# A hybrid S5 and mLSTM decoder block: rotation tables of the state space built once for all columns, and two steps of VectorE's work on ScalarE

## The chip, the core and the metric

The kernel runs on one core of a Trainium2 chip, as one launch. The metric is the device time of one execution in microseconds. The median of three executions before the change is 1532.45 us (1532.4 to 1532.74). In the profile the engines are PE (TensorE), with its weight loads listed apart as PEld, DVE (VectorE), ACT (ScalarE), POOL (GpSimd) and SP (SyncE, which here issues nearly all DMAs). They run side by side and wait for one another through semaphores; each takes its own instructions in the order in which they were written into its queue.

## What is computed

One decoder block over 16 meta tokens and 1024 tokens, width 1024, float32 throughout:

```python
h = layer_norm(concat([meta, x]), ln0_g, ln0_b)
p = h @ w_in + b_in
u_s5, q, k, v, o_pre, i_pre, f_pre, g_s5, g_m = split(p)
z = gelu(s5_mixer(u_s5)) @ s5_w_glu
y_s5 = z[..., :D] * sigmoid(z[..., D:])
qk = silu(causal_depthwise_conv(concat([q, k]), qk_conv_w, qk_conv_b))
hm = head_norm(mlstm(q_h, k_h, v_h, i_pre, f_pre), m_norm_g)
y_m = (sigmoid(o_pre) * hm) @ m_w_out
mix = sigmoid(g_s5) * y_s5 + sigmoid(g_m) * y_m
h = layer_norm(alpha * h + mix @ w_o)
ff = relu(h @ w_up + b_up) ** 2 @ w_down
h = layer_norm(alpha * h + ff)
return h[N_META:]
```

The S5 mixer is a diagonal complex recurrence, x_t = A x_(t-1) + B u_t, for 32 groups of 64 states. The convolution has four taps. head_norm takes each head's 256 values, subtracts their mean and divides by their deviation.

## The kernel before

**Matmuls.** A product of two float32 matrices is made of three passes over rounded halves (mm3, lines 240 to 242): high by high, low by high, high by low. So every weight block is loaded by SP (load_w, L206), rounded to a high half whi on ACT (L220), and its remainder wlo is computed on DVE (L221). Both halves come out of split_now, which split_w wraps in a priority with the offset SPLIT_UP (0 here). The activations stand in SBUF as hT_hi and hT_lo.

**The order of the work.** The string ORDER lists the projection jobs: q0 stands for the two jobs q and k of head 0, v0 for its values, o for output gates, u for the four blocks of S5 inputs, g for gates of S5, e0 for the first pair of mLSTM gates. Jobs run one after another on PE; while one runs, it asks (job.after) for the next weights to be split, after its first block, or, for a v job, after the chunk VAFT (0). Work that doesn't belong to a job runs in lanes: generators that do a few operations and then yield a length of time. After every second term of a product pump moves a nominal clock on, and every lane whose time has come does its next step. A lane's pace in PACE and the lists ML, NL, C5, K5, Z5, D5, W5 and Y5 (one number for each head or batch) stretch or shorten these yields. So they set where, between which matmuls, small work of the lanes is written. A scheduler then orders each engine's queue by priority and a simulated timeline, so that neighbours in the code may change places on an engine. S5_START names the job at which the S5 preparation is put in its lane, LANE_AT those at which t_prep (sums and halves of the normalised input), hm_gate (heads times output gates), ah_scale (the residual scaled) and up_early (early halves of the up projection) are.

**SBUF.** Most buffers of 1056 columns come from one pool of 30 slots (slot). A load or a step that needs a slot waits until an earlier user is done.

**The q and k jobs.** After its matmuls each puts conv_steps in the lane cv: the first tap with the bias is one DVE operation (L330), three more taps (L333) add to it on DVE, then come a sigmoid on ACT (L336) and a product. There are eight such rows of 1040 columns.

**The heads.** mlstm(h) works in nine chunks. A(c) makes the scores pS on PE and their weighted copy sw on DVE (L499); B(c) makes the outputs pn and the state update pu, and writes the row's output to hraw on ACT (L530). After four chunks N takes the four reciprocal deviations (rsqrt), subtracts the mean and scales 256 columns four times on DVE (L540), transposes on PE (L547) and stores through ACT (L548).

**The state space.** s5_pre computes constants for all 16 columns of states: powers E of A, r8 (the size of A to the eighth) and p8 (its angle as cosine and sine), and B's scaled form bb. s5_consts(b) makes, for each batch b of four columns, the matrices of the chunked recurrence: Pt and the transposes Mi, Rr and Ri, the kernel Kt (matmuls s5k), RS and Mx. Last it makes a table T: cosine and sine of n steps of rotation, n = 0 to 129, for four columns. Each level doubles the part that is known by a complex product (cmul, six operations, L608 to L613) on DVE, from 1 column each to 64 and then the last one: eight levels. s5_batch(b) takes the inputs (matmuls s5z), rotates them by T, runs eight scans, rotates back and makes the outputs s5y; s5_gelu(b) makes the halves that the first glu job reads. That job begins by draining the lanes s5c, s5 and s5g.

Of the kernel before, what the change touches and what calls it, by code (L numbers as in the profile page):

```python
# [9 lines left out]
F32 = mybir.dt.float32  # L10
F32R = mybir.dt.float32r
I32 = mybir.dt.int32
AF = mybir.ActivationFunctionType
OP = mybir.AluOpType
P = 128
# [5 lines left out]
LEN = SEQ + META  # L21
# [16 lines left out]
LN2_1 = 0.693359375  # L38
LN2_2 = math.log(2.0) - LN2_1
MAGIC = 1.5 * 2 ** 23  # L40
ORDER = 'q0 q1 v0 v1 q3 o1 q2 o2 v2 o0 o3 u0 u1 v3 u2 g0 u3 o4 o6 o5 o7 g1 g6 g3 e0 g5 g2 g7 g4'
S5_START = 'o3'
LANE_AT = {'t_prep': 'q3', 'hm_gate': 'u3', 'ah_scale': 'g2', 'up_early': 'g7'}
PACE = {'ml': 0.56, 'cv': 1.742, 's5': 1.0, 's5c': 1.0, 's5g': 1.6, 'ah': 1.936, 'up': 1.764, 'hg': 1.25}
SPLIT_UP = 0
PRE = 3
ZD = 1
ML = [2.64, 1.32, 1.497, 5.28]
NL = [0.563, 2.188, 2.188, 1.54]
C5 = [0.7, 0.98, 1.568, 0.517]  # L50
K5 = [1.7, 2.72, 1.87, 1.7]
Z5 = [1.0, 0.681, 0.75, 1.0]
D5 = [2.333, 0.889, 0.7, 0.42]
W5 = [2.407, 1.912, 3.54, 4.425]
Y5 = [2.597, 2.115, 2.028, 2.115]
AFT = 0
VAFT = 0
LOAD0 = "x0 c0 w0 x1 w1 c1 x2 w2 x3 w3 x4 x5 x6"
LN0_PROG = " ".join((
# [61 lines left out]
def decoder_block(  # L121
# [5 lines left out]
    v_, a_, g_, t_ = nc.vector, nc.scalar, nc.gpsimd, nc.tensor  # L127
# [5 lines left out]
    mid = mid_ctx.enter_context(tc.tile_pool(name="mid", bufs=1, side="left"))  # L133
# [3 lines left out]
    def slot(name, dt=F32):  # L137
        return big.tile([P, SLOT], dt, tag="s", name=name)
# [12 lines left out]

    lanes = {n: Lane(p) for n, p in PACE.items()}
    clock = [0.0]
# [20 lines left out]
    convt = const.tile([P, 8, 5], F32, name="convt")  # L174
    mngt = const.tile([P, 8], F32, name="mngt")

    def rsqrt(var, n, pre, pool):
        y = pool.tile([P, 16], F32, tag="rs_y", bufs=4, name=pre + "y")[:, :n]
        u = pool.tile([P, 16], F32, tag="rs_u", bufs=4, name=pre + "u")[:, :n]
        a_.activation(y, var, AF.Sqrt, bias=eps_t[:, 0:1])  # L180
        v_.reciprocal(y, y)
        v_.scalar_tensor_tensor(u, var, EPS, y, op0=OP.add, op1=OP.mult)
        v_.scalar_tensor_tensor(u, u, -0.5, y, op0=OP.mult, op1=OP.mult)
        v_.scalar_tensor_tensor(y, u, 1.5, y, op0=OP.add, op1=OP.mult)
        return y
# [23 lines left out]
    def split_w(job, later=False):  # L209
        if later:  # L210
            return split_now(job, True)
        with tc.high_priority(offset=SPLIT_UP):
            split_now(job)
# [101 lines left out]
    def qk_job(h, isk):  # L315
        st = {}
        ci = h + 4 * isk

        def evac(bi, c0, c1, ps):
            if "pre" not in st:  # L320
                st["pre"] = slot("cpre")
                v_.memset(st["pre"][:, 0:3], 0.0)
            a_.activation(st["pre"][:, 3 + c0:3 + c1], ps, AF.Identity, bias=bft[:, JQ + ci:JQ + ci + 1])

        def done():
            lanes["cv"].add(conv_steps(st["pre"]))

        def conv_steps(pre):
            y = slot("cy")
            v_.tensor_scalar(y[:, :LEN], pre[:, 0:LEN], convt[:, ci, 0:1], convt[:, ci, 4:5],  # L330
                             op0=OP.mult, op1=OP.add)
            for w in range(1, 4):
                v_.scalar_tensor_tensor(y[:, :LEN], pre[:, w:w + LEN], convt[:, ci, w:w + 1], y[:, :LEN],  # L333
                                        op0=OP.mult, op1=OP.add)
                yield 1.2
            a_.activation(pre[:, :LEN], y[:, :LEN], AF.Sigmoid)  # L336
            yield 1.2
            r = slot("kT" if isk else "qT")
            v_.scalar_tensor_tensor(r[:, :LEN], y[:, :LEN], DK ** -0.5 if isk else 1.0, pre[:, :LEN],
                                    op0=OP.mult, op1=OP.mult)  # L340
            QK[h, isk] = r
            yield 0.5
        fm_job(JQ + ci, BLK0[len(all_jobs)] if len(all_jobs) < 4 else BLK, 0, evac, done)
# [122 lines left out]
    def mlstm(h):  # L466
# [9 lines left out]
        for c in range(NCH):  # L476
            c0, n = chunk(c)
# [56 lines left out]
        def N(half, hm):  # L534
            hraw, mv = hm
            y = rsqrt(mv[:, :, 1], 4, "hn", mid)
            yield NL[h]
            for i in range(4):
                hr = hraw[:, i * DV:(i + 1) * DV]
                v_.tensor_scalar(hr, hr, mv[:, i, 0:1], y[:, i:i + 1], op0=OP.subtract, op1=OP.mult)  # L540
            yield NL[h]
            for f in range(2):
                if half == 0:
                    HM[2 * h + f] = slot("hmF")
                ps = sdps("pt")
                for i in range(4):
                    t_.transpose(ps[:, i * P:(i + 1) * P], hraw[:, i * DV + f * P:i * DV + (f + 1) * P], ident)  # L547
                a_.activation(HM[2 * h + f][:, half * 512:(half + 1) * 512], ps, AF.Copy,  # L548
                              scale=mngt[:, 2 * h + f:2 * h + f + 1])
                if half == 1:  # L550
                    nc.sync.dma_start(hm_dr[2 * h + f], HM.pop(2 * h + f)[:, :D])
                    DONE.add(2 * h + f)
                yield 1.2
# [3 lines left out]
        for c in range(NCH):  # L557
            if c + 1 < NCH:
                A(c + 1)
            yield ML[h]  # L560
            B(c)
            yield ML[h]
            if c == 5:
# [24 lines left out]
    S5, UD = {}, set()  # L588
# [18 lines left out]
    def cmul(eng, orr, oi, ar, ai, br, bi, t1, t2):  # L607
        eng.tensor_tensor(t1, ar, br, op=OP.mult)  # L608
        eng.tensor_tensor(t2, ai, bi, op=OP.mult)
        eng.tensor_tensor(orr, t1, t2, op=OP.subtract)  # L610
        eng.tensor_tensor(t1, ar, bi, op=OP.mult)
        eng.tensor_tensor(t2, ai, br, op=OP.mult)
        eng.tensor_tensor(oi, t1, t2, op=OP.add)  # L613

    def s5_pre():
# [47 lines left out]
        p8 = mid.tile([P, 2, 16], F32, name="s5_p8")  # L663
# [9 lines left out]
        for n in (1, 2, 4):  # L673
            sh = [P, n, 16]
            w1 = tm[:, 0:n * 16].rearrange("p (a b) -> p a b", b=16)
            w2 = tm[:, 256:256 + n * 16].rearrange("p (a b) -> p a b", b=16)
# [20 lines left out]
        sh = [P, 16, 16]  # L697

        def v3(ap):
# [4 lines left out]
             wr[:, :, None].to_broadcast(sh), wi[:, :, None].to_broadcast(sh),  # L704
             v3(tm[:, 0:256]), v3(tm[:, 256:512]))
        yield 1.3

    GEL = {}

    def s5_consts(b):  # L710
        E, ER = S5["E"], S5["ER"]
        q0 = 4 * b
# [11 lines left out]
        sh = [P, 4, 8, 16]  # L724
# [8 lines left out]
        g_.tensor_tensor(t2, bi, ei, op=OP.mult)  # L733
        yield C5[b]
        g_.tensor_tensor(pr, t1, t2, op=OP.subtract)
        g_.tensor_tensor(t1, br, ei, op=OP.mult)
        yield C5[b]
        g_.tensor_tensor(t2, bi, er, op=OP.mult)
        g_.tensor_tensor(pi, t1, t2, op=OP.add)
        yield C5[b]  # L740
        sh = [P, 4, 9, 16]
        Rr, Ri, tm = slot("s5Rr"), slot("s5Ri"), slot("s5tm")
        tm2 = slot("s5tm")
        cr, ci = (C4(r)[:, :, None, :].to_broadcast(sh) for r in (0, 1))
# [4 lines left out]
        v_.tensor_tensor(t2, ci, ei, op=OP.mult)  # L749
        yield C5[b]  # L750
        v_.tensor_tensor(rr, t1, t2, op=OP.subtract)
        v_.tensor_tensor(t1, cr, ei, op=OP.mult)
        yield C5[b]
        v_.tensor_tensor(t2, ci, er, op=OP.mult)
        v_.scalar_tensor_tensor(Ri[:, 0:576], tm[:, 0:576], -1.0, tm2[:, 0:576], op0=OP.mult, op1=OP.subtract)
        yield C5[b]
        BD = [Rr[:, 576:704].rearrange("p (q g h) -> p q g h", q=4, h=16),
              Rr[:, 704:832].rearrange("p (q g h) -> p q g h", q=4, h=16)]
        g_.memset(Rr[:, 576:832], 0.0)
        for ri in range(2):  # L760
            for g2 in range(2):
                s = slice(64 * g2, 64 * g2 + 64)
# [29 lines left out]
        for j in range(8):  # L792
            for g2 in range(2):
                nc.sync.dma_start(mx[16 * j:16 * j + 16, :, g2, 16 * j:P],
                                  kt[16 * g2:16 * g2 + 16, :, 0:P - 16 * j])
        yield K5[b]
        T = slot("s5T")
        tc_, ts_ = (T[:, i * 520:(i + 1) * 520].rearrange("p (q c) -> p q c", q=4) for i in range(2))
        tmp = slot("s5tt")
        g_.memset(tc_[:, :, 0], 1.0)  # L800
        g_.memset(ts_[:, :, 0], 0.0)
        g_.tensor_copy(tc_[:, :, 1], S5["p8"][:, 0, q0:q0 + 4])
        g_.tensor_copy(ts_[:, :, 1], S5["p8"][:, 1, q0:q0 + 4])
        yield C5[b]
        n = 1
        while n < 129:
            m = min(n, 129 - n)
            sh = [P, 4, m]
            w1 = tmp[:, 0:4 * m].rearrange("p (q c) -> p q c", q=4)
            w2 = tmp[:, 512:512 + 4 * m].rearrange("p (q c) -> p q c", q=4)  # L810
            cmul(v_, tc_[:, :, n + 1:n + 1 + m], ts_[:, :, n + 1:n + 1 + m], tc_[:, :, 1:m + 1], ts_[:, :, 1:m + 1],
                 tc_[:, :, n:n + 1].to_broadcast(sh), ts_[:, :, n:n + 1].to_broadcast(sh), w1, w2)
            n *= 2
            yield C5[b]
        S5["m", b] = (RS, Mi, Mx, T)

# [543 lines left out]

    for w in ORDER.split():
        n, i = w[0], int(w[1:])
# [29 lines left out]
    for w in LOAD0.split():  # L1392
        i = int(w[1])
# [27 lines left out]
    for i, j in enumerate(jobs):  # L1421
# [11 lines left out]
        for lane, name, gen in (("ah", "t_prep", t_prep), ("hg", "hm_gate", hm_gate), ("ah", "ah_scale", ah_scale),  # L1433
                                ("up", "up_early", up_early)):
            if j.tag == LANE_AT[name]:
                lanes[lane].add(gen())
# [15 lines left out]
    for k in range(KT):  # L1452
        r = slot("woraw")
# [570 lines left out]
```

## Time and profile before

| what | us |
|---|---|
| median of the runs | 1532.45 |
| the profiled execution | 1531.35 |
| its span, first to last instruction | 1529.6 |
| PE busy | 1512.4 |
| DVE busy | 1065.9 |
| ACT busy | 623.4 |
| POOL busy | 107.3 |

Busy time of PE is modelled: matmuls overlap, and a matmul of 512 columns is listed with some 390 ns though the next one starts after 230. So a busy PE doesn't say that it is at its peak, but an idle PE is time lost. A stretch of the timeline is read by the distance between starts. "Waits" put an engine's idle time down to the instruction that released it. Behind each line of the page that groups instructions stand the count, busy time and mean ns of one, then the idle time of the engine just before them.

### The profile page before, as it was taken

What the parts mean: (1) busy time and instruction counts of PE and PEld (TensorE: products, weight loads), DVE (VectorE), ACT (ScalarE), POOL (GpSimd) and SP (SyncE); (2) the same over time, 40 slices, a digit from 0 to 9 for tenths busy, and PEclk for the clock granted to TensorE, in tenths of its full rate; (3) what the DMA queues carried; (4) which work ended last, traced back from release to release, by engine and by line L of the source; (5) the groups of instructions that cost most, each with busy time, mean ns of one, the idle gap of its engine ahead of it and who ended that gap; (6) DMA issues with size and microseconds to landing.
All of it is one profiled execution on the core that took longest, in us unless ns stands there. A gap on an engine that the chain in (4) does not pass through costs nothing.

```text
span 1529.6 us, 20808 instructions
## 1 busy us (share of the span) xinstructions
PE 1512.4 (99%) x7652; PEld 1280.4 (84%) x7652; DVE 1065.9 (70%) x2054; ACT 623.4 (41%) x994; POOL 107.3 (7%) x180
## 2 busy tenths in 40 slices
PE   9999999999999999999999999999999999999997
PEld 9999988998888888888878887888888888888886
DVE  7568775689868667674348575766666689767786
ACT  6624544424255352343025253444444533433440
POOL 0000000624122000010000001000000000000000
PEclk9999999999999999999999999999999999999999
DMA  9403655504762999796352247644443897667642
GB/s 332 147 9 98 190 160 164 167 23 125 245 212 76 329 321 360 289 314 218 109 195 94 97 132 247 193 152 148 148 149 132 278 381 278 232 242 232 209 179 97
DMA packets 155256, 294.51 MB, mean 193 GB/s; under 512 B 19001, under 2 KB 69633, under 8 KB 155153
## 3 DMA queue, kind: packets, MB, share of 16 engines
q1 hardware_dynamic: 147776, 273.77, 52.8%
q0 software_dynamic: 7376, 19.40, 4.1%
q8 instruction: 60, 0.98, 0.3%
q14 instruction: 44, 0.35, 0.1%
HBM read 196.39 MB, written 95.56 MB: 191 GB/s over the span
## 4 chain that ended last, share of the span: by engine, by line
PE 65%; issue 27%; DVE 4%; DMA 2%; ACT 1%; POOL 0%; POOLq 0%; SPq 0%; DVEq 0%; ACTq 0%
PE mm L240 16%; PE mm L242 16%; PE mm L241 16%; PE sd L241 3%; PE sd L240 3%; PE sd L242 3%; PE mm L236 2%; PE mm L274 1%; PE pu L511 1%; PE pn L507 1%; PE pn L508 1%; PE warm L1281 1%; DMA wpre<-wu_dr 1%; DMA gB<-grow_dr 1%; PE ln L1255 0%
## 5 line engine op out<-in xcount | busy, mean ns | idle before, releaser
L240 PE MATMUL mm<-hT_hi,whi 128*128 128x512 f32 (+3 forms) x480 | 181.4, 378 | 0.0
L242 PE MATMUL mm<-hT_hi,wlo 128*128 128x512 f32 (+3 forms) x480 | 179.0, 375 | 1.3 <-DVE wlo L221 1.2
L241 PE MATMUL mm<-hT_lo,whi 128*128 128x512 f32 (+3 forms) x480 | 177.6, 370 | 0.0
L242 PEld LDWEIGHTS mm<-hT_hi,wlo 128*128 128x128 f32 x480 | 90.8, 189 | 14.1 <-DVE wlo L221 2.0
L241 PEld LDWEIGHTS mm<-hT_lo,whi 128*128 128x128 f32 x480 | 90.8, 189 | 12.7 <-issue 0.9
L240 PEld LDWEIGHTS mm<-hT_hi,whi 128*128 128x128 f32 x480 | 90.7, 189 | 12.1 <-issue 0.2
L221 DVE TENSOR_TENSOR wlo<-wraw,whi 128x1024 fp32r<-128x1024 f32 (+1 forms) x56 | 69.4, 1248 | 41.4 <-ACT whi L220 26.7
L1719 ACT ACTIVATE dah<-da 128x1024 fp32r<-128x1024 f32 x56 | 58.7, 1051 | 87.5 <-PE sd L241 37.1
L241 PE MATMUL sd<-dwl,dah 128*128 128x512 f32 x240 | 94.3, 393 | 0.0
L240 PE MATMUL sd<-dwh,dah 128*128 128x512 f32 x240 | 94.2, 393 | 0.0
L242 PE MATMUL sd<-dwh,dal 128*128 128x512 f32 x240 | 94.0, 392 | 0.0
L1723 ACT ACTIVATE dwh<-wdr 128x1024 fp32r<-128x1024 f32 x56 | 58.9, 1054 | 80.6 <-DMA wdr<-in_wdn_dram 28.9
L220 ACT ACTIVATE whi<-wraw 128x1024 fp32r<-128x1024 f32 (+1 forms) x56 | 58.4, 1054 | 64.2 <-PE mm L242 18.8
L240 PE MATMUL mm<-dwh,dah 128*128 128x512 f32 (+1 forms) x224 | 84.5, 378 | 0.0
L242 PE MATMUL mm<-dwh,dal 128*128 128x512 f32 (+1 forms) x224 | 84.4, 377 | 0.0
L241 PE MATMUL mm<-dwl,dah 128*128 128x512 f32 (+1 forms) x224 | 84.3, 377 | 0.0
L1720 DVE TENSOR_TENSOR dal<-da,dah 128x1024 fp32r<-128x1024 f32 x56 | 68.1, 1220 | 22.4 <-ACT dah L1719 21.8
L1724 DVE TENSOR_TENSOR dwl<-wdr,dwh 128x1024 fp32r<-128x1024 f32 x56 | 68.2, 1219 | 11.4 <-ACT dwh L1723 10.8
L240 PE MATMUL mm<-whi,hT_hi 128*128 128x256 f32 (+1 forms) x256 | 74.6, 291 | 0.0
L241 PE MATMUL mm<-wlo,hT_hi 128*128 128x256 f32 (+1 forms) x256 | 73.6, 287 | 0.0
L242 PE MATMUL mm<-whi,hT_lo 128*128 128x256 f32 (+1 forms) x256 | 73.4, 287 | 0.0
L240 PE MATMUL mm<-th,wuh 128*128 128x512 f32 x156 | 61.6, 395 | 0.0
(475 smaller groups left out, 3890.4 us busy)
## 6 DMA issues: line engine op xcount, KB each, us to landing
da<-act_dr SPq DMA_DIRECT2D x56, 512.0 KB, 5.2
wdr<-in_wdn_dram SPq DMA_DIRECT2D x56, 512.0 KB, 6.2
wraw<-in_wf_dram SPq DMA_DIRECT2D x32, 512.0 KB, 5.7
wur<-in_wup_dram SPq DMA_DIRECT2D x32, 512.0 KB, 4.3
act_dr<-upy SPq DMA_DIRECT2D x64, 256.0 KB, 2.6
wu_dr<-wpre SPq DMA_DIRECT2D x21, 512.0 KB, 6.3
wpre<-wu_dr POOLq DMA_DIRECT2D x21, 512.0 KB, 4.9
t_dr<-tpo SPq DMA_DIRECT2D x16, 512.0 KB, 4.6
```

Source lines behind the costliest of these rows:

```text
L220: a_.activation(hi[:, :n], r[:, :n], AF.Copy)
L221: todo.append(lambda e=v_, r=r, hi=hi, lo=lo, n=n: e.tensor_tensor(lo[:, :n], r[:, :n], f32(hi[:, :n]), op=OP.subtract))
L236: t_.matmul(ps, tm[i], tm[j], start=(w == 0 and k == 0), stop=(w == 2 and k == n - 1))
L240: t_.matmul(ps, ah, bh, start=(i == 0 and part[0]), stop=False, skip_group_check=skip)
L241: t_.matmul(ps, ah, bl, start=False, stop=False, skip_group_check=skip)
L242: t_.matmul(ps, al, bh, start=False, stop=(i == n - 1 and part[1]), skip_group_check=skip)
L274: t_.matmul(ps[:, :P], job.first[:, k * P:(k + 1) * P], HF[c0 // P][:, k * P:(k + 1) * P], start=(k == 0), stop=(k == KT - 1))
L507: t_.matmul(pn[:, :257], qi[:, c0:c0 + n], Cs[c][:, :257], start=True, stop=False)
L1719: a_.activation(ah[:, :D], a[:, :D], AF.Copy)
L1720: v_.tensor_tensor(alo[:, :D], a[:, :D], f32(ah[:, :D]), op=OP.subtract)
L1723: a_.activation(wh, raw[i], AF.Copy)
L1724: v_.tensor_tensor(wl, raw[i], f32(wh), op=OP.subtract)
```

## The change

The table of rotations is split. s5_pre now also builds 33 steps for all 16 columns at once, by five levels on DVE and the 33rd step on POOL, and keeps them in one slot. s5_consts copies a batch's columns from there on POOL, and only two levels of doubling, of 32 and 64 columns, are left in each batch. The complex product and its temporaries are in a new function rotate.

The first tap of the convolution is done by ACT (CV0 = 1). In N, two of each four scalings go to ACT (HRA = 1), as scale and bias; the bias, minus mean times reciprocal deviation, is one more small DVE operation for each N.

SPLIT_UP becomes 50, so that weight splits are ranked up to 50 places ahead of their position, and VAFT becomes 3. In ORDER o3 stands ahead of o0, e0 near the end, and o4 to o7 and some g jobs change places. t_prep joins its lane at o1, ah_scale at the first glu job. Paces and yields change.

```diff
-ORDER = 'q0 q1 v0 v1 q3 o1 q2 o2 v2 o0 o3 u0 u1 v3 u2 g0 u3 o4 o6 o5 o7 g1 g6 g3 e0 g5 g2 g7 g4'
+ORDER = 'q0 q1 v0 v1 q3 o1 q2 o2 v2 o3 o0 u0 u1 v3 u2 g0 u3 o5 g1 o4 g6 o6 o7 g3 g5 g7 g4 e0 g2'
 S5_START = 'o3'
-LANE_AT = {'t_prep': 'q3', 'hm_gate': 'u3', 'ah_scale': 'g2', 'up_early': 'g7'}
-PACE = {'ml': 0.56, 'cv': 1.742, 's5': 1.0, 's5c': 1.0, 's5g': 1.6, 'ah': 1.936, 'up': 1.764, 'hg': 1.25}
-SPLIT_UP = 0
+LANE_AT = {'t_prep': 'o1', 'hm_gate': 'u3', 'ah_scale': 'glu', 'up_early': 'g7'}
+PACE = {'ml': 0.56, 'cv': 0.737, 's5': 1.0, 's5c': 1.0, 's5g': 1.6, 'ah': 1.549, 'up': 1.764, 'hg': 0.66}
+SPLIT_UP = 50
...
-ML = [2.64, 1.32, 1.497, 5.28]
-NL = [0.563, 2.188, 2.188, 1.54]
-C5 = [0.7, 0.98, 1.568, 0.517]
-K5 = [1.7, 2.72, 1.87, 1.7]
-Z5 = [1.0, 0.681, 0.75, 1.0]
-D5 = [2.333, 0.889, 0.7, 0.42]
-W5 = [2.407, 1.912, 3.54, 4.425]
-Y5 = [2.597, 2.115, 2.028, 2.115]
+ML = [2.904, 1.32, 1.318, 5.28]
+NL = [0.558, 2.166, 1.3, 1.372]
+C5 = [0.693, 0.97, 2.485, 0.307]
+K5 = [1.02, 2.72, 1.496, 1.87]
+Z5 = [1.125, 0.851, 0.938, 1.25]
+D5 = [2.333, 0.889, 0.7, 0.374]
+W5 = [2.383, 1.704, 3.505, 4.38]
+Y5 = [2.828, 2.303, 2.209, 2.303]
 AFT = 0
-VAFT = 0
+CV0 = 1
+HRA = 1
+VAFT = 3
...
-            v_.tensor_scalar(y[:, :LEN], pre[:, 0:LEN], convt[:, ci, 0:1], convt[:, ci, 4:5],
-                             op0=OP.mult, op1=OP.add)
+            if CV0:
+                a_.activation(y[:, :LEN], pre[:, 0:LEN], AF.Identity, scale=convt[:, ci, 0:1], bias=convt[:, ci, 4:5])
+            else:
+                v_.tensor_scalar(y[:, :LEN], pre[:, 0:LEN], convt[:, ci, 0:1], convt[:, ci, 4:5],
+                                 op0=OP.mult, op1=OP.add)
...
             y = rsqrt(mv[:, :, 1], 4, "hn", mid)
+            nm = mid.tile([P, 16], F32, tag="rs_m", bufs=2, name="hnm")[:, :4]
+            v_.scalar_tensor_tensor(nm, mv[:, :, 0], -1.0, y, op0=OP.mult, op1=OP.mult)
             yield NL[h]
             for i in range(4):
                 hr = hraw[:, i * DV:(i + 1) * DV]
-                v_.tensor_scalar(hr, hr, mv[:, i, 0:1], y[:, i:i + 1], op0=OP.subtract, op1=OP.mult)
+                if HRA & (1 << (i % 2)):
+                    a_.activation(hr, hr, AF.Identity, scale=y[:, i:i + 1], bias=nm[:, i:i + 1])
+                else:
+                    v_.tensor_scalar(hr, hr, mv[:, i, 0:1], y[:, i:i + 1], op0=OP.subtract, op1=OP.mult)
...
         yield 1.3
+        rot = slot("s5rot")
+        tmr = slot("s5tm")
+        S5["rot"] = R = rot[:, 0:1056].rearrange("p (r q c) -> p r q c", r=2, q=16)
+        v_.tensor_copy(R[:, :, :, 0], p8)
+        for n in (1, 2, 4, 8, 16):
+            rotate(v_, R[:, 0], R[:, 1], n, n, tmr, 16)
+            yield 1.3
+        rotate(g_, R[:, 0], R[:, 1], 32, 1, tmr, 16)
...
+    def rotate(eng, c, s, n, m, tmp, nq):
+        sh = [P, nq, m]
+        w1 = tmp[:, 0:nq * m].rearrange("p (q c) -> p q c", q=nq)
+        w2 = tmp[:, 512:512 + nq * m].rearrange("p (q c) -> p q c", q=nq)
+        cmul(eng, c[:, :, n:n + m], s[:, :, n:n + m], c[:, :, 0:m], s[:, :, 0:m],
+             c[:, :, n - 1:n].to_broadcast(sh), s[:, :, n - 1:n].to_broadcast(sh), w1, w2)
...
-        g_.tensor_copy(tc_[:, :, 1], S5["p8"][:, 0, q0:q0 + 4])
-        g_.tensor_copy(ts_[:, :, 1], S5["p8"][:, 1, q0:q0 + 4])
+        g_.tensor_copy(tc_[:, :, 1:34], S5["rot"][:, 0, q0:q0 + 4])
+        g_.tensor_copy(ts_[:, :, 1:34], S5["rot"][:, 1, q0:q0 + 4])
         yield C5[b]
-        n = 1
-        while n < 129:
-            m = min(n, 129 - n)
-            sh = [P, 4, m]
-            w1 = tmp[:, 0:4 * m].rearrange("p (q c) -> p q c", q=4)
-            w2 = tmp[:, 512:512 + 4 * m].rearrange("p (q c) -> p q c", q=4)
-            cmul(v_, tc_[:, :, n + 1:n + 1 + m], ts_[:, :, n + 1:n + 1 + m], tc_[:, :, 1:m + 1], ts_[:, :, 1:m + 1],
-                 tc_[:, :, n:n + 1].to_broadcast(sh), ts_[:, :, n:n + 1].to_broadcast(sh), w1, w2)
-            n *= 2
+        for n, m in ((33, 32), (65, 64)):
+            rotate(v_, tc_[:, :, 1:130], ts_[:, :, 1:130], n, m, tmp, 4)
             yield C5[b]
```

## The prediction

> **What bounds the kernel now.** I read the page first: which engine fills the span.
>
> ```profile
> span 1529.6 us, 20808 instructions
> PE 1512.4 (99%) x7652; PEld 1280.4 (84%) x7652; DVE 1065.9 (70%) x2054; ACT 623.4 (41%) x994; POOL 107.3 (7%) x180
> ```
>
> TensorE (PE) is busy for 1512.4 of 1529.6 us, and the change removes no matmul. All that an edit to the other engines can win is time in which PE stands still or runs slowly: 17.2 us over the span. The second view, busy time by stretch (from, to, length; busy us and count of PE, weight loads, DVE, ACT, POOL; granted clock, DMA share, GB/s), says where in the stretches that hold the state space (S5) part:
>
> ```profile
> 120.00:240.00 120.00, 119.81 (x750) 111.25 (x749) 91.80 (x239) 56.75 (x90) 5.36 (x12) 1.00 0.48 143
> 240.00:360.00 120.00, 119.59 (x753) 109.21 (x752) 85.99 (x273) 47.78 (x80) 38.80 (x63) 1.00 0.39 120
> 360.00:480.00 120.00, 116.38 (x606) 98.75 (x604) 98.88 (x258) 51.56 (x79) 33.91 (x37) 0.99 0.57 184
> 480.00:600.00 120.00, 120.00 (x565) 98.82 (x563) 87.73 (x169) 52.97 (x73) 3.95 (x8) 1.00 0.84 294
> ```
>
> Of these 480 us PE loses 0.19, 0.41, 3.62 and nothing. So 360 to 480 us is the only place with something to win, and there DVE is at its fullest (98.88 of 120). The view of waits, PE's alone from 200 to 480 us, names what it waited for (total, times, longest):
>
> ```profile
> PE s5z L838 <- DVE sw L499: 1.4, 1, 1.4
> PE mm L242 <- DVE wlo L221: 1.2, 1, 1.2
> PE s5k L776 <- DVE sw L499: 0.5, 1, 0.5
> PE s5p L769 <- ACT s5Y L897: 0.3, 1, 0.3
> PE s5p L769 <- ACT hmF L548: 0.3, 1, 0.3
> PE pt L547 <- DVE hraw L540: 0.2, 1, 0.2
> ```
>
> They sum to 3.9 us. The two largest wait for DVE, and the chain of waits over the same stretch shows what DVE was doing (start, length, what):
>
> ```profile
> 367.34 1.14 DVE wlo L221
> 368.48 1.01 DVE s5tt L608
> ```
>
> After the late weight half wlo comes the first, tiny operation of a rotation table, and it takes a microsecond. The timelines of DVE and POOL, rows picked, say why:
>
> ```profile
> 364.50 2.83 DVE L781 SCALAR_TENSOR_TENSOR s5Kt<-s_eye,s_d,s5Kt 32x16 f32<-32x16 f32 x4
> ...
> 368.40 1.09 DVE L608 TENSOR_TENSOR s5tt<-s5T 128x4 f32<-128x4 f32 x1
> ...
> 377.76 0.29 DVE L499 TENSOR_TENSOR sw<-pS,gB 128x128 f32<-128x128 f32 x1
> 364.53 2.35 POOL L483 TENSOR_TENSOR qi<-qT,wiB 128x1024 f32<-128x1024 f32 x1 [5.04 <-DVE s5w L882]
> ...
> 374.30 1.30 POOL L739 TENSOR_TENSOR s5P<-s5tm 128x512 f32<-128x512 f32 x1
> ```
>
> While POOL works, from 364.53 to 375.6, DVE's small operations stretch. The scores product sw, which frees the PSUM bank that s5z needs, stands in DVE's queue behind 23 of them (four levels of 6, less one), from 368.40 to 377.76: 9.4 us.
>
> The stall has a tail. PE's timeline and the busy times of two small stretches, in the same columns as above:
>
> ```profile
> 378.67 0.69 PE L242 MATMUL mm<-hT_hi,wlo 128*128 128x400 f32 x1
> 379.15 0.54 PE L240 MATMUL mm<-hT_hi,whi 128*128 128x400 f32 x1
> ...
> 381.81 0.39 PE L242 MATMUL mm<-hT_hi,wlo 128*128 128x400 f32 x1
> 382.04 0.34 PE L240 MATMUL mm<-hT_hi,whi 128*128 128x400 f32 x1
> 382.22 0.34 PE L241 MATMUL mm<-hT_lo,whi 128*128 128x400 f32 x1
> 375.08:378.48 3.40, 1.96 (x11) 1.30 (x10) 3.06 (x17) 0.21 (x1) 0.52 (x1) 1.00 0.11 15
> 378.48:381.90 3.42, 3.42 (x14) 3.42 (x13) 3.15 (x14) 1.10 (x2) 0.00 (x0) 0.50 0.62 161
> ```
>
> Behind the stall the granted clock is 0.50 for 3.42 us. Matmuls of 400 columns then start every 0.33 us (eight steps from 379.15 to 381.81) instead of every 0.18 (382.22 - 382.04), which loses 8 x 0.15 = 1.2, and the step from 378.67 to 379.15 loses another 0.3: 1.5 us.
>
> **The change part by part, against the profiled execution.** That took 1531.35 us (span 1529.6 and 1.75 around it), 1.10 below the median of 1532.45, so I add 1.10 at the end.
>
> *Rotation tables.* DVE's work on s5tt, one window for each batch:
>
> ```profile
> 316.20:334.20 18.00, 12.22 (x48) 1.00 0.03 5
> 368.40:386.30 17.90, 14.93 (x48) 0.90 0.47 150
> 429.49:446.00 16.51, 9.38 (x48) 1.00 0.44 124
> 480.00:501.70 21.70, 9.42 (x48) 1.00 0.43 135
> ```
>
> Each batch has 8 levels of 6 operations. It keeps two levels, 12 operations of 128 and 256 columns, and loses 36. In the quiet batches (9.4) the kept levels are the long ones, by this row under 0.43 us each, so at most 5.2 of 9.4; at least 4 us goes in a quiet batch, and in the second one the 30 operations of the first five levels (368.40 to 379.49) go out of the disturbed stretch. Added, once: 30 operations and a copy in s5_pre on 16 to 256 columns, bounded by 0.15 us (the smallest) and 0.43 each, 5 to 13 us, spread over six steps of the lane some 100 us ahead, in the stretch 240 to 360 where DVE has 34 us free and PE waits for little. Price on PE's path: nothing; without that cover, at most the 13 us. Six more operations for the 33rd step and two wider copies in each batch go to POOL:
>
> ```profile
> L681 POOL COPY s5E<-s5E x8: 208/238/377, 262.5 to 275.2; 128x32 f32<-128x32 f32 x8
> L802 POOL COPY s5T<-s_p x4: 189/404/1266, 299.0 to 480.5; 128x4 f32<-128x4 f32 x4
> ```
>
> A copy of 132 columns isn't in the trace; 0.2 (L681) to 1.3 us (L802 at worst) each, I take 0.4. DVE waits for it as it already waits for the 4-column copy; behind that wait stand sw and wlo, so a batch could lose up to 2.2 us more and most likely loses nothing, for POOL is idle 93% of the span.
>
> *Gain.* sw ended at 378.05 and PE had waited 1.4 for it. Without the 23 operations it runs up to 9.4 us sooner, as soon as its scores are there: the wait goes, and the 1.5 of slow clock behind it: -2.9. The wait of 1.2 for wlo stands behind L781 and the first batch's own chain, which starts earlier when its table loses 36 operations; SPLIT_UP = 50 also lets weight splits pass up to 50 priority places of other work. Bounds 0 to -1.2; I take -1.2.
>
> *First tap and half the head scaling to ScalarE.*
>
> ```profile
> L330 DVE TENSOR_SCALAR cy<-cpre,convt x8: 803/818/821, 68.1 to 196.9; 128x1040 f32<-128x1040 f32 x8
> L540 DVE TENSOR_SCALAR hraw<-hraw,hmv,hny x32: 402/409/2534, 164.5 to 488.4; 128x256 f32<-128x256 f32 x32
> L530 ACT ACTIVATE hraw<-pn,dd 128x256 f32<-128x256 f32 x32 | 15.1, 471 | 61.5 <-DVE dd L529 47.7 <-PE pu L511 7.8 <-DMA s5yc<-ys_dr 3.0
> L220 ACT ACTIVATE whi<-wraw x56: 1039/1051/1081, 13.9 to 777.3; 128x1024 fp32r<-128x1024 f32 x54, 128x1056 fp32r<-128x1056 f32 x2
> ```
>
> DVE loses 8 x 0.82 and 16 x 0.41, 13.1 us, and gains eight tiny products; ACT gains 8 x about 1.07 (L220 scaled to 1040) and 16 x 0.47, 16.1 us, where it is under half busy. Almost all lies where PE waits for nothing (before 240 us it loses 0.19). Only the last wait of the list, 0.2 for hraw, can go: -0.2. The added wait is DVE's second tap on ACT's first; behind it in DVE's queue are sw and v rows, and ACT's whole cost of 1.07 would be its price if uncovered.
>
> *Order, paces, moved steps.* o3 now stands before o0, so s5_pre starts one job earlier; its added steps pay for that. e0 moves to the end with its two weight loads and its stores; its readers come eight jobs later. ah_scale moves to glu with 10 loads, 8 stores and 18 DVE operations past the last gates on SP's queue; its rows are read after all of the mixing. VAFT = 3 makes the v jobs ask for the next split three chunks later. I price these at nothing on PE's path while the loads land early, but a new order of queues leaves new small waits. I take one like s5k's 0.5 and one like s5p's 0.3: +0.8.
>
> **Sum:** -2.9 - 1.2 - 0.2 + 0.8 = -3.5; 1531.35 - 3.5 = 1527.85, and 1.10 to the median: **1528.9 us**.
>
> **The rivals.** *All waits go:* the 3.9 us of the list and 1.5 of clock, no new ones: 1532.45 - 5.4 = 1527.0. For it: every releaser on the list is relieved but s5Y and hmF; against it: those are ACT's, which gets more work.
>
> *The stall moves:* DVE's queue is written by the scheduler, which put sw behind 9.4 us of other work; it can put it behind the hm_gate products instead, whose pace falls from 1.25 to 0.66. The same 1.4 and 1.5 come back: 1528.95 + 2.9 = 1531.9. For it: the order in the queue isn't written out by hand here; against it: 9.4 us of work is a rare lump.
>
> *The slow clock isn't the stall's.* By the Trainium skill, TensorE: Matmul & The Clock Gate, Part 1 (The HAM clock gate), the clock is halved after a window of about 3.4 us without activity; the idle stretch here is shorter. The trace differs (clock 0.50 behind a window 1.96 of 3.40 busy), and I follow it. As a mechanism of this kernel: if the 3.42 us at 0.50 comes whatever the queue does, 1.5 of the gain stays away: 1530.4.
>
> *A weight load comes too late: slower.* The table of all 16 columns holds one of 30 slots from s5_pre to the last batch, some 200 us, and SP's queue is in order:
>
> ```profile
> SPq L206 <- DVE s5T L613: 14.7, 1, 14.7
> 357.79 0.38 SPq L206 DMA_DIRECT2D wraw<-in_wf_dram  x1
> wraw<-in_wf_dram SPq DMA_DIRECT2D x32, 512.0 KB, 5.7
> 371.81 1.05 ACT L220 ACTIVATE whi<-wraw 128x1024 fp32r<-128x1024 f32 x1
> ```
>
> Already a load (L206) waits 14.7 us for a slot. The one issued at 357.79 would land at 363.5 by the median of 5.7 and is split at 371.81: 8.3 us to spare. From there on lateness decides; a slot that comes one load later than that costs 5.7 and 1.5 of clock, keeps the wlo wait (no -1.2) and leaves -2.9: 1532.45 + 7.2 - 2.9 = 1536.7. Against it: the table's temporary is now freed sooner.
>
> **How the numbers follow.** Forecast 0.45; all waits go 0.10; the stall moves 0.20; the clock 0.05; the late load 0.20. A difference of 0.2%, 3.1 us, is about what a measurement of this kernel can tell from no change, so faster means below 1529.4: 0.45 + 0.10 = 0.55; within 0.25; slower 0.20. The likeliest's own range is 1527.0 (all waits) to 1530.4 (clock). The range asked for goes down another 2.5, an allowance of about half the 5.4 for matmuls that start late while PE counts as busy, to 1524.5, and up past the late load to 1537.5.
>
> **What would show it.** Right: s5tt with 12 operations in each batch; sw within 2 us of its scores in the second batch; no stretch at clock 0.50 between 300 and 500 us; PE idle from 360 to 480 under 2 us. Wrong: PE waits for wlo or sw of more than 1 us there, a wraw load that lands after its split could have started, or PE waiting for cy, hraw or gell.

## The result, and the profile after

The changed kernel takes 1535.38 us (median of nine, 1533.77 to 1539.3) beside 1532.11 for the kernel before in the same session; the ratio is 1.0025, 95% interval 1.0014 to 1.0035. So it is slower by 3.3 us, and the interval lies wholly above 1; the forecast was 3.5 us faster. The profiled execution took 1534.25 us with a span of 1532.5, beside 1531.35 and 1529.6 before, so it shows 2.9 us of it. First the page's totals of the changed kernel (busy us, share of the span, count):

```profile
span 1532.5 us, 20740 instructions
PE 1513.1 (99%) x7652; PEld 1280.2 (84%) x7652; DVE 1037.5 (68%) x1925; ACT 637.6 (42%) x1016; POOL 109.4 (7%) x186
```

DVE lost 28.4 us of work and ACT took on 14.2, which is what the edit is for. The span grew all the same. The busy times by stretch, in the columns of the prediction, say where:

```profile
240.00:360.00 120.00, 118.19 (x751) 108.28 (x751) 87.31 (x268) 49.67 (x86) 39.55 (x69) 1.00 0.38 117
360.00:480.00 120.00, 115.16 (x614) 96.94 (x613) 88.31 (x198) 53.96 (x91) 35.70 (x41) 0.99 0.58 184
480.00:600.00 120.00, 120.00 (x540) 98.02 (x539) 68.18 (x105) 53.27 (x69) 3.05 (x4) 1.00 0.81 286
```

PE's loss in 240 to 360 us rose from 0.41 to 1.81, in 360 to 480 from 3.62 to 4.84: 2.6 us together, nearly all of the 2.9. In the second of these stretches DVE works 10.6 us *less* than before (88.31 beside 98.88), and PE still waits more. PE's waits from 100 to 800 us (total, times, longest):

```profile
PE s5p L794 <- DVE C L521: 1.8, 1, 1.8
PE mm L244 <- DVE wlo L223: 1.7, 3, 1.0
PE s5z L856 <- DVE C L521: 1.4, 1, 1.4
PE pn L512 <- DVE C L521: 1.0, 1, 1.0
PE s5z L856 <- DVE sw L504: 0.4, 1, 0.4
PE s5z L856 <- DVE s5Z L864: 0.3, 1, 0.3
PE pt L557 <- DVE C L521: 0.2, 1, 0.2
```

They sum to 6.8 us; the kernel before has 4.1 in the same window (the 3.9 of the prediction and 0.2 more). Of the two largest waits of before, the one for sw is gone and the one for wlo is left, for the same weight half (1.0 us at 370, 1.2 before). 4.4 of the 6.8 are for something that PE did not wait for before: the update of the mLSTM's state C (128 x 257, L521), an operation of 0.47 us which reads the product pu and so frees its PSUM bank.

**The first new wait, at 346 us.** The timelines of DVE and PE of the changed kernel (start, length; in brackets the idle time before it and what ended it):

```profile
338.67 3.54 DVE L882 TENSOR_TENSOR_SCAN s5w<-s_r,s5Z 128x130 f32<-128x130 f32 x6
...
346.34 0.47 DVE L521 SCALAR_TENSOR_TENSOR C<-C,dec,pu 128x257 f32<-128x257 f32 x1
342.16 0.59 PE L516 MATMUL pu<-v,kw 128*128 128x257 f32 x2
346.95 0.63 PE L794 MATMUL s5p<-ident,s5P 128*128 128x128 f32 x4 [1.75 <-DVE C L521]
```

The product pu is done at 342.75, and its C (head 2, chunk 7) starts 3.6 us later, behind the scans and products of the first S5 batch. In the kernel before the two did not meet; its DVE timeline has that C 17 us ahead of the scans:

```profile
335.63 0.47 DVE L516 SCALAR_TENSOR_TENSOR C<-C,dec,pu 128x257 f32<-128x257 f32 x1
352.96 3.44 DVE L864 TENSOR_TENSOR_SCAN s5w<-s_r,s5Z 128x130 f32<-128x130 f32 x8
```

The batch's chain came 14 us earlier (352.96 to 338.67) and the head's end 11 us later (335.63 to 346.34): they passed each other. Neither shift alone would have brought them together: a C at 335.63 is still ahead of scans at 338.67, and one at 346.34 ahead of scans at 352.96.

**The last new wait, at 473 us, with a tail.** DVE's, PE's and SP's timelines, rows picked:

```profile
473.57 1.23 DVE L962 TENSOR_TENSOR hgr<-hgr,hgo 128x1024 f32<-128x1024 f32 x1 [5.96 <-DMA hgo<-og_dr]
474.71 0.48 DVE L521 SCALAR_TENSOR_TENSOR C<-C,dec,pu 128x257 f32<-128x257 f32 x1
475.25 0.71 PE L856 MATMUL s5z<-s5U,s5Mi 128*128 128x130 f32 x4 [1.37 <-DVE C L521]
456.56 10.23 SPq L819 DMA_DIRECT2D s5Mx<-s5Kt  x16
...
468.48 0.38 SPq L958 DMA_DIRECT2D hgo<-og_dr  x1
```

DVE stands idle for 5.96 us. Its next instruction is a gate product of hm_gate whose operand hgo is still being loaded, since SP's queue had 16 small loads of s5Mx ahead of it for 10.23 us. C (head 3, chunk 6) is behind that product, and PE's s5z behind C. The busy times of the window with this stall and of the one behind it:

```profile
473.69:477.10 3.41, 1.77 (x9) 1.14 (x9) 3.22 (x6) 0.72 (x3) 0.00 (x0) 1.00 0.99 402
477.10:480.51 3.41, 3.41 (x13) 3.04 (x13) 2.37 (x9) 2.40 (x8) 0.00 (x0) 0.50 0.90 301
```

The slow clock that stood at 378.48 before stands at 477.10 now. At half speed 3.41 us of PE's work cost at most 1.7 us more; the prediction counted 1.5 for such a window.

### The profile page after: what moved, and what is told of

Its sections match the earlier page's. It is cut to its first block, busy times and chain, and to the rows that moved or that the text cites. A ratio compares the mean times of both kernels' runs of the same rounds, so it can differ in the third digit from the quotient of the medians.

```text
span 1532.5 us, 20740 instructions
## 1 busy us (share of the span) xinstructions
PE 1513.1 (99%) x7652; PEld 1280.2 (84%) x7652; DVE 1037.5 (68%) x1925; ACT 637.6 (42%) x1016; POOL 109.4 (7%) x186
## 4 chain that ended last, share of the span: by engine, by line
PE 76%; issue 16%; DVE 4%; DMA 3%; SPq 1%; ACT 0%; POOLq 0%; POOL 0%; DVEq 0%
PE mm L244 20%; PE mm L243 20%; PE mm L242 20%; PE sd L242 3%; PE sd L243 3%; PE sd L244 3%; PE mm L238 2%; DMA hgo<-og_dr 1%; PE mm L276 1%; PE pu L516 1%; PE pn L512 1%; DMA wraw<-in_wf_dram 1%; PE pn L513 1%; PE warm L1299 1%; SPq L819 1%
```

## The experiments

Each kernel was timed against the kernel before on one chip; ratios are to that kernel, with their 95% intervals. The changed kernel itself stands at 1.0025. The expectations speak of theories by letters. A: the faster pace of hm_gate puts products that wait for their loads ahead of C. B: the first batch's chain, now earlier, stands ahead of C. D: both kernels are narrowly set, and whatever deals the queues anew costs, with the paces fitted to the table. Other letters stand for one part of the change that costs by itself; each expectation says which.

**hm_gate's pace as before.**

```diff
-PACE = {..., 'hg': 0.66}
+PACE = {..., 'hg': 1.25}
```

> The changed kernel with one number put back: the pace of hm_gate, 0.66 to 1.25. Theory A (head of line: hm_gate's products L962 stand in DVE's queue before their hgo rows have landed, and the state update C behind them makes PE wait 1.0 us at 416 and 1.4 us at 473, with 3.4 us of clock 0.50 behind the second): these two waits and the slow clock go, 4 us, so about 1531.4 us, 0.9993 of before. Theory B (the first batch's S5 chain, now earlier, stands before head 2's C at 346 us, 1.8 us): that wait stays and the time falls by no more than A's part. Theory C (the shared table's slot makes weight loads late): nothing changes, 1.0025. Theory D (any edit reorders the scheduler's queues, and the sum of small waits moves by some 3 us either way): waits appear at other places, 1530 to 1537 us.

Measured: 1535.37 us, ratio 1.0027 (1.0016 to 1.0038). The waits at 416 and 473 us and the stretch at clock 0.50 are gone, but not the 4 us that theory A put on them. The three largest of PE's waits:

```profile
PE mm L244 <- DVE wlo L223: 4.5, 5, 2.5
PE s5p L794 <- DVE C L521: 1.7, 1, 1.7
PE pu L516 <- ACT hraw L535: 1.3, 1, 1.3
```

The wait at 346 us stays, and late weight halves (4.5 us) take the place of the others. The faster pace does make the wait at 473 us; putting the pace back is worth nothing.

**The table alone, and everything but the table.** The first is the kernel before with s5_pre's 33 steps, rotate and the two levels in s5_consts, and none of the other edits. The second is the changed kernel with the old eight levels.

> The kernel before with the table built once for all columns and nothing else changed (order, paces, first tap and head scaling as before). The prediction's step: sw no longer behind 23 small operations, so the waits of 1.4 for sw and 1.2 for wlo and 1.5 us of slow clock go, 1528 to 1530 us, 0.997 to 0.999. Theory B: the S5 chain of the first batches comes some 10 us earlier and meets head 2's or head 3's work, so new waits for C of 1 to 3 us eat the gain, 0.999 to 1.002. Theory C (slot): waits for wlo whose load landed late, above 1.002.

> The changed kernel with the old table code (eight levels in each batch), everything else as changed. If the table is the cause of the loss (B or C), this is at or below before, 1529 to 1532 us, 0.998 to 1.000. If order, paces and hm_gate are (A), it is as slow as the changed kernel or slower, since DVE has some 28 us more work: 1535 to 1540, 1.002 to 1.005.

Measured: 1565.21 us, 1.0217 (1.0203 to 1.0231), and 1555.54, 1.0156 (1.0142 to 1.017). The three largest of PE's waits with the table alone:

```profile
PE mm L242 <- DVE wlo L221: 4.9, 3, 2.5
PE mm L240 <- ACT whi L220: 4.8, 3, 2.4
PE s5z L847 <- DMA s5U<-us_dr: 4.5, 1, 4.5
```

By itself the table, which takes work off DVE, costs 33 us with the old paces; everything else with the old table costs 24; together they cost 3. The second time lies above every range that was expected. The first does but for theory C's open one, and C is not the reason: the two whi that PE waits for there started 36 and 29 us after their loads had landed. So neither part can be judged without the other, and a part's cost can't be read from leaving it out.

**Without ACT's new work.**

```diff
-CV0 = 1
-HRA = 1
+CV0 = 0
+HRA = 0
```

> The changed kernel with first tap and head scaling back on DVE (CV0 = 0, HRA = 0). By all theories these lie where PE waits for nothing: 1.002 to 1.003 as the changed kernel. If ACT's added work were the cause, 1.000 or below. By theory D any place within 1530 to 1538 us.

Measured: 1536.28 us, 1.0029 (1.0017 to 1.004), with C waited for 1.9 and 1.6 us at the same two places as in the changed kernel (1.8 and 1.4). The move to ACT neither costs nor gains anything that can be told.

**The first batch's last constants held back.** In s5_batch, ahead of the point where RS, Mi, Mx and T are taken:

```diff
+        if b == 0:
+            yield 12.0
```

> The changed kernel with 12 us of lane time put before the first S5 batch begins (once its constants are there). Theory B (the shorter table lets the first batch's rotations and scans run some 10 us earlier, in the middle of head 2's chunks, where the state update C and the weight half wlo wait behind them): the waits of 1.8 us for C at 346 and of 0.4 for wlo at 383 go, the time falls by about 2 us to 1533. Theory D (each edit only deals the same small waits anew): other waits of 1 to 2 us take their place, 1533 to 1538.

Measured: 1545.81 us, 1.0093 (1.0077 to 1.0108). That is above both ranges. The wait at 346 us is gone, as theory B has it: C of head 2, chunk 7 runs at 333.20 us, not at 346.34, and the batch's scans from 359.12. This speaks for the early batch having held up the head's end too. This wait, of 8 us, is new:

```profile
PE s5y L914 <- DVE s5w L902: 8.0, 1, 8.0
```

**A yield after every two scans** instead of one for all, with their sum the same.

```diff
         for q in range(4):
...
-        yield D5[b]
+            yield D5[b] / 4
```

> The changed kernel with the eight scans of a batch written in four steps of two with a quarter of the yield between them, instead of one step. Theory E (the lump: what makes PE wait is that one lane step puts 3.4 to 4.1 us of DVE work ahead of C or wlo in DVE's queue): the 1.8 us at 346 and the 0.4 at 383 shrink by more than half, 1532.5 to 1534 us, 0.9995 to 1.0015. Theory D: no change in sum, 1.002 to 1.004.

Measured: 1543.39 us, 1.0077 (1.0063 to 1.0091), above both ranges. DVE's order around 346 us did not change, since the scheduler and not the yield sets it there: PE still waits 1.7 us for C. Elsewhere wlo is late by 8.5 us in all. That says nothing on the wait at 346 us.

**SPLIT_UP back to 0.**

> The changed kernel with SPLIT_UP back at 0. By the prediction's step the offset of 50 brings wlo earlier; then without it waits for wlo grow by 1 to 3 us: 1536.5 to 1538.5, 1.003 to 1.005. If the offset is itself the harm (weight halves pushed ahead of C), the waits for C shrink and the time falls to 1532 to 1534.

Measured: 1536.32 us, 1.0027 (1.0016 to 1.0037), with wlo late by 2.8 us instead of 1.7. The priority of weight splits is not the cause.

**A nudge of the kernel before.** One yield of one batch, 5% longer, and nothing else.

```diff
-C5 = [0.7, 0.98, 1.568, 0.517]
+C5 = [0.7, 1.03, 1.568, 0.517]
```

> The kernel before with one number moved by 5%: the second batch's yield in C5, 0.98 to 1.03; same work. Theory D: the queues are dealt anew and the time lands 1 to 5 us away from before, mostly above: 1.001 to 1.004. If only real work counts, 1.000 (within 0.05%).

Measured: 1550.64 us, 1.0125 (1.0111 to 1.0139). Its two largest waits:

```profile
PE mm L242 <- DVE wlo L221: 6.4, 3, 4.5
PE s5y L894 <- DVE s5w L882: 4.0, 1, 4.0
```

18.5 us from a step that changes no work, where theory D expected 1 to 5: one such nudge moves the time by several times what the change was to bring. So experiments that move a lane can't separate the causes here. The last five take single operations off DVE's queue and leave the order of the rest as nearly as can be. For a chosen update of C:

```diff
+                    if (h, c) in ((2, 7),):
+                        g_.tensor_scalar(Cs[c + 1][:, :257], Cs[c][:, :257], dec[:, c:c + 1], None, op0=OP.mult)
+                        cu = mid.tile([P, 258], F32, tag="cu", bufs=1, name="cu")
+                        a_.activation(cu[:, :257], pu[:, :257], AF.Copy)
+                        g_.tensor_tensor(Cs[c + 1][:, :257], Cs[c + 1][:, :257], cu[:, :257], op=OP.add)
```

**One update of C (head 2, chunk 7).** PE's order and that of DVE's other instructions are the same as in the changed kernel.

> The changed kernel, but one update of the state C of 128x257 (head 2, chunk 7, the one that PE's step s5p waits 1.75 us for at 346.95 us) leaves DVE's queue: ScalarE copies pu out of PSUM (0.47 us by its copies of 256 columns) and GpSimd scales C and adds. The order of PE's queue and of DVE's other operations stays as it was. Theory 'the gain was given back in new waits for single operations that stand behind other work in DVE's queue': the wait of 1.75 goes, nothing else changes, 1535.4 - 1.75 = 1533.6, ratio to the kernel before 1.0010 to 1.0015. Rival 'what the wait loses isn't on the path, or the next wait takes its place': the ratio stays at 1.0025 and another wait of 1 to 2 us appears within 30 us of it.

Measured: 1531.05 us, 0.9992 (0.9983 to 1.0001): 0.33% less than the changed kernel, about 5 us where 1.75 was expected. The profiled executions show 2.0 us of this (spans 1532.5 and 1530.5). The two largest of its waits:

```profile
PE s5z L862 <- DVE C L527: 3.8, 1, 3.8
PE mm L242 <- ACT whi L222: 1.2, 1, 1.2
```

And of DVE's and POOL's timelines:

```profile
339.48 2.01 DVE L888 TENSOR_TENSOR_SCAN s5w<-s_r,s5Z 128x130 f32<-128x130 f32 x6
472.71 1.23 DVE L968 TENSOR_TENSOR hgr<-hgr,hgo 128x1024 f32<-128x1024 f32 x1 [8.40 <-DMA hgo<-og_dr]
344.06 0.74 POOL L525 TENSOR_TENSOR C<-C,cu 128x257 f32<-128x257 f32 x1 [4.84 <-ACT cu L524]
344.74 2.10 POOL L816 COPY s5RS<-s5Rr 64x512 f32<-64x512 f32 x2
```

The wait at 346 us went, and those at 368, 383 and 416 us went with it. Part of what the rival said came too: the 1.2 for whi, at 352.4 us, is new. This whi ran at nearly the same time in the changed kernel (351.12 there, 351.33 here), where PE came too late to wait for it. One side effect: POOL waited for the copy cu with the s5RS copies behind it, so these no longer ran beside the scans, and six scans took 2.01 us instead of 3.54. This did not end the batch's chain sooner: its last product (s5w) ends at 349.4 us here and at 349.2 in the changed kernel, since the copies now run beside the products. What comes sooner is the next head: DVE starts on its gates' 128-column steps (gB) at 357.16 us instead of 359.41, on the second table at 359.01 instead of 361.25, and on the wlo behind that table at 366.05 instead of 368.73. The expected 1.75 covers only the wait itself; that the later ones hang on it was not foreseen. At the gate product the stall grew to 3.8 us: PE comes there earlier, and the load of hgo, though issued 4.3 us earlier (464.20 beside 468.48), lands hardly earlier. It took 8.4 us to land here and 5.0 in the changed kernel.

**A second update of C (head 3, chunk 6).** As above, for (2, 7) and (3, 6).

> As the one before it, and a second update of C (head 3, chunk 6: at 473.5 us it stands behind a gate product that waits 5.96 us for its load, PE's s5z waits 1.37 us for it, and 3.41 us at clock 0.50 follow) goes to ScalarE and GpSimd too; PE's order changes in a dozen places around it. Theory of the waits: 1533.6 - 1.37 - 1.5 (slow clock) = 1530.7, ratio 0.999 (0.998 to 1.000), and no stretch of clock 0.50 between 300 and 500 us. Rival (the next wait takes its place): ratio 1.001 or above, because the gate product that waits for its load still holds DVE's queue for 6 us and something else behind it is waited for, the copies of s5z first.

Measured: 1533.8 us, 1.0009 (1.0 to 1.0018): a miss for the theory of the waits; its rival is close on the time and right on the place. The first line of its waits:

```profile
PE s5z L862 <- DVE s5Z L870: 4.6, 1, 4.6
```

DVE's timeline has

```profile
472.25 1.23 DVE L968 TENSOR_TENSOR hgr<-hgr,hgo 128x1024 f32<-128x1024 f32 x1 [8.58 <-DMA hgo<-og_dr]
```

and the busy times of the stretch behind it are

```profile
473.55:480.38 6.83, 5.17 (x16) 4.53 (x17) 5.72 (x15) 3.63 (x9) 0.00 (x0) 0.50 0.76 268
```

With C out of the way PE waits for the copy of s5z, which stands behind the same gate product; the slow clock lasts two windows (6.83 us). The instruction that is waited for is not the cause; the one at the head of the queue is.

**And a late half (gell) on GpSimd.** As above, and in s5_gelu:

```diff
-        v_.tensor_tensor(lo[:, 0:1024], gf[:, 0:1024], f32(hi[:, 0:1024]), op=OP.subtract)
+        (g_ if b == 0 else v_).tensor_tensor(lo[:, 0:1024], gf[:, 0:1024], f32(hi[:, 0:1024]), op=OP.subtract)
```

> As the one before it, and the low half of the first batch's gelu output (gell, 128x1024, at 414.85 us, 2.18 us on DVE with the update of C for head 3, chunk 2 behind it, for which PE's pn waits 1.04 us at 416.4) is computed on GpSimd. Theory of the waits: 1530.7 - 1.04 = 1529.7, ratio 0.9983. Rival: GpSimd's 2 to 3 us on 1024 columns stand ahead of the first products of the next batch (s5tm, 414.85 now), whose chain comes later, and stretch DVE's small operations meanwhile: ratio 0.999 to 1.001, with a new wait for s5p or wlo between 415 and 440 us.

Measured: 1532.81 us, 1.0007 (0.9998 to 1.0016), not told apart from the one before it; the wait that it aimed at had already gone with (2, 7).

**The gate product itself, with (2, 7).**

```diff
-                v_.tensor_tensor(a[:, :D], a[:, :D], b[:, :D], op=OP.mult)
+                (g_ if f == 6 else v_).tensor_tensor(a[:, :D], a[:, :D], b[:, :D], op=OP.mult)
```

> The changed kernel with two operations moved off DVE's queue: the update of C for head 2, chunk 7 (to ScalarE and GpSimd, as before), and the sixth gate product (hgr of 128x1024, which held DVE's queue for 8.40 us while its load landed, with the update of C and the copies of s5z behind it), which goes to GpSimd, idle from 453.6 us to the end of the state-space part. Theory of the waits: of the kernel with the first operation moved alone (1531.05) the wait of 3.8 us goes, and the 3.41 us at clock 0.50 behind it (1.5): 1525.8, ratio 0.9959 (0.995 to 0.997), with PE idle from 360 to 480 us under 1.5. Rival (every wait that is taken away is replaced by the next one): ratio 0.998 to 1.000 and a new wait of 3 us or more between 440 and 500 us.

Measured: 1528.46 us, 0.9976 (0.9968 to 0.9985), faster than both kernels: 3.4 us below the kernel before, 0.49% below the changed one. All of PE's waits from 100 to 800 us:

```profile
PE mm L242 <- ACT whi L222: 1.2, 1, 1.2
PE mm L244 <- DVE wlo L223: 0.5, 2, 0.3
PE s5z L862 <- DVE sw L504: 0.4, 1, 0.4
```

POOL's timeline with the product, which now waits there while nothing stands behind it (the bracket names s5z, but the load of hgo landed at 469.55, just ahead of it):

```profile
469.71 2.40 POOL L968 TENSOR_TENSOR hgr<-hgr,hgo 128x1024 f32<-128x1024 f32 x1 [16.26 <-PE s5z L862]
```

And the busy times from 360 to 480 us:

```profile
360.00:480.00 120.00, 119.22 (x642) 101.59 (x641) 91.72 (x201) 56.24 (x93) 39.94 (x42) 1.00 0.60 186
```

PE loses 0.78 us there instead of 4.84, and the clock stays at 1.00. Against the changed kernel the span fell by 7.0 us (1532.5 to 1525.5): the waits account for 4.7 (6.8 to 2.1) and the slow clock for 1.5 to 1.7. A few instructions of PE and DVE near the product changed places as well. The time is 2.7 above the expected 1525.8 and the ratio close to the rival's 0.998, but what the rival asks for, a new wait of 3 us or more, is not there. Against the kernel with (2, 7) alone the spans fell by 5.0 us (1530.5 to 1525.5), as expected, and the medians by 2.6: that kernel's profiled execution, with its stall of 3.8, is one of its longer ones (1532.28 beside the median of 1531.05), and this one's is one of its shorter (1527.32). The load of hgo took 8.4 us there and 4.5 here, so some of the 5.0 us may be the load's scatter.

**The gate product alone.**

> The changed kernel with only the sixth gate product on GpSimd; the update of C for head 2, chunk 7 stays behind the first batch's chain on DVE. Theory of the waits: the wait of 1.37 us at 473 and the slow clock behind it go, the others stay: 1535.4 - 2.9 = 1532.5, ratio 1.0005. If the wait at 346 pushes the later ones (368, 383, 416), as their going along with it suggested, they are still there, 1.0, 0.4 and 1.0 us. Rival (replaced): ratio 1.002 or above.

Measured: 1530.9 us, 0.999 (0.9981 to 0.9998), where the theory of the waits had 1532.5 and the rival 1.002 or above. Lines of its waits:

```profile
PE mm L244 <- DVE wlo L223: 2.0, 3, 1.3
PE s5p L794 <- DVE C L521: 1.8, 1, 1.8
PE pt L557 <- ACT hraw L548: 1.3, 1, 1.3
PE pn L512 <- DVE C L521: 0.7, 1, 0.7
```

The wait at 473 us and its slow clock are gone, though the product started only at 476.65 us on POOL, because its load took 8.6 us. The waits at 346, 368, 383 and 416 us still stand (1.8, 1.3, 0.5 and 0.7), and one of 1.3 for hraw at 498 us is new. So the earlier group hangs on the update of C (or on the copies that moved with it) and not on the gate product, and each of the two operations is worth about 5 us alone by the medians (0.33% and 0.35%, each uncertain by some 2 us) and 7.5 together (0.49%). The profiled executions show 2.0, 1.4 and 7.0 (those of the single moves are among the longer of their kernels, and the changed kernel's among its shorter). It is shown that each is worth something and that both together beat the kernel before; how much each is worth alone is not. Nor is it shown whether their gains overlap, as the longer wait at the gate product without the first one (3.8 us beside 1.37) suggests.

## Why the prediction was wrong

**The new order of queues, +0.8: this step failed.** It allowed for two small waits, and priced the moved steps at nothing "while the loads land early". By the two profiles this term came to 5.5: new waits of 5.1 (4.4 for C, 0.4 for sw, 0.3 for s5Z) and 1.5 of slow clock behind the last stall, less the 1.1 that went with the waits at s5k and s5p. The rest of the sum came to -2.9 for sw and its clock, +0.3 for wlo and -0.2 for hraw, so +2.7 in all; the spans differ by 2.9. The prediction looked at how much work DVE loses and not at which instruction would stand ahead of which. C came to stand behind the first batch's chain and behind a gate product whose load had not landed. Taking two instructions off DVE's queue brings 1528.46, 3.4 below the kernel before where the forecast had 3.5. That agreement is luck, of the sum alone: the extra edits moved the s5RS copies too, and left other waits than the forecast's.

**sw and its slow clock, -2.9: right for the stall, and taken up elsewhere.** Each batch runs 12 operations for its table, eight per line in four batches:

```profile
L618 DVE TENSOR_TENSOR s5tt<-s5T x8: 259/350/1220, 315.7 to 458.5; 128x128 f32<-128x128 f32 x4, 128x256 f32<-128x256 f32 x4
```

The wait at 376 us and the slow clock behind it are gone. sw did not come within 2 us of its scores, as the prediction had asked: in the second batch it ran 3.2 us behind them (377.45 to 380.67), but PE had other work.

**wlo, -1.2: not gained in the changed kernel.** Three waits for wlo cost 1.7 us, beside 1.4 in all before. The largest, 1.0 us, is for the same weight half as the 1.2 before. It now stands behind the second batch's table, whose kept levels are stretched beside POOL's products (0.42 us each when POOL is idle):

```profile
365.58 1.52 DVE L619 TENSOR_TENSOR s5tt<-s5T 128x256 f32<-128x256 f32 x1
...
368.73 1.22 DVE L223 TENSOR_TENSOR wlo<-wraw,whi 128x1024 fp32r<-128x1024 f32 x1
```

With (2, 7) off the queue the two waits at 370 and 384 us are gone. The reason given, that the first batch's chain starts earlier, came true, and that same start put the scans ahead of C and, by the run that held the batch back, held up the head's end. What was counted as a gain caused the first new wait.

**hraw, -0.2:** gone from its place (207 us). A wait of 0.2 for C came up at another head's transposes, at 457 us.

**ACT's work at no cost: right in effect, low in size.** A first tap takes 1.25 us on ACT and one scaling of 256 columns 0.59, where 1.07 and 0.47 were assumed:

```profile
L333 ACT ACTIVATE cy<-cpre,convt 128x1040 f32<-128x1040 f32 x8 | 10.0, 1250 | 0.1
L548 ACT ACTIVATE hraw<-hraw,hnm,hny 128x256 f32<-128x256 f32 x16 | 8.7, 592 | 9.3 <-DVE hnm L543 9.3
```

Putting both back to DVE changed nothing that can be told (1.0029 beside 1.0025).

**The rivals.** *The stall moves* was right in mechanism and even in place: C, if not sw, stood behind an hm_gate product, with pace 0.66, and the slow clock followed. It was priced as one stall, 2.9 us, for a time of 1531.9; the pace put back removed it, and brought others of the same size. What it lacked is that there were several stalls at once. *The slow clock isn't the stall's* falls: it left 378 us with the stall, came back at 477 us behind another, and is absent from 300 to 500 us with hm_gate's pace put back and in both kernels with the gate product on POOL. *A late weight load* was not seen: PE waits for no whi in the changed kernel. Its margin was read too large, though: the load issued at 357.79 us took 9.1 us, not 5.7, so 4.9 us were to spare and not 8.3. The load that did come late was the gates' hgo. *All waits go* did not come about; with the two operations moved 2.1 us of waits are left.

What stays open: why single steps cost as much as they do (18.5 us for 5% of one yield) was not traced through the scheduler. How the waits at 368 to 416 us hang on the first one is settled only in part: the traces speak for the next head's gates, which come 2.2 us sooner, and not for the shorter scans, but no run moves one without the other.

## What to carry to other kernels

On an engine that is only 70% busy, an edit is judged by the order of its queue: ask of each instruction that waits for a load or belongs to a long chain what stands behind it, and whether PE needs that. Where a scheduler deals the queues, measure first what a nudge that changes no work does; here it was five times the expected gain, so parts could be told apart only by taking single instructions off a queue and leaving the others. When a wait's releaser is taken away and the wait stays, look at the head of that queue.

## What the runs showed of the hardware

The same idle time does not always bring the slow clock. Windows of the changed kernel, counted back in steps of 3.41 us from 477.10, where the clock fell (the two falls of the kernel with the first batch held back are 88.75 us apart, 26 such steps):

```profile
343.98:347.39 3.41, 1.66 (x13) 1.31 (x12) 3.40 (x10) 0.60 (x1) 0.00 (x0) 1.00 0.17 40
347.39:350.81 3.42, 3.42 (x27) 2.83 (x26) 2.68 (x10) 1.61 (x4) 1.05 (x4) 1.00 0.63 194
```

Here PE is busy for 1.66 of 3.41 us and the next window runs at 1.00; at 473.69 it is busy for 1.77 of 3.41 and the next runs at 0.50. Counted so in all 15 profiles, from 100 to 620 us, at full clock, the 14 windows with PE busy for under 1.2 us were all followed by a slow one, and none with over 2.0 us was; of the 19 between 1.48 and 1.97, five were. What tells these apart is open. By the Trainium skill, TensorE: Matmul & The Clock Gate, Part 1 (The HAM clock gate), the clock falls after an idle window of about 3.4 us; both windows hold less idle time than that, so the fall at 477.10 came sooner than this rule has it.

POOL's copies of 64 x 512 stretch DVE's work beside them: six scans of 130 columns took 3.54 us with the copies and 2.01 without. A product of 128 x 1024, 1.23 us on DVE, took 2.40 on POOL, and scaling 257 columns there 1.77 where DVE scales and adds in 0.47.
